# A decoder layer whose up projection uses pairs with seven products: another order of a pair's splits and products, and other distances between the additions and relus that close a column chunk

## The chip, the cores and the metric

The kernel runs on one core of one Trainium2 chip. The metric is the device time of the core in microseconds (us). Before the change it is 1089.05 us, the median of three runs (1088.41 to 1090.12).

## The reference, cut to what matters

One decoder layer on x of 256 tokens x 2048 channels, in float32:

```python
h = rmsnorm(x) * norm_attn_pre
p = h @ w_in                       # q, k, v of A; two latents and the shared key of B
A = dilated_window_attention(...)  # 8 heads of 128
B = causal_attention(...)          # 8 heads, from the latents by w_uq and w_ukv
x = x + rmsnorm(concat(A, B) @ w_out) * norm_attn_post
h = rmsnorm(x) * norm_mlp_pre
u = square(relu(h @ w_up))         # 2048 -> 8192
x = x + rmsnorm(u @ w_down) * norm_mlp_post   # 8192 -> 2048
```

The change lies in the line with w_up.

## The kernel before, in words

**Exact products from parts.** Every float32 operand is split into two parts of TensorE's format, `hi` (rounded by ScalarE, L268, or L272 where a gain is multiplied in) and `lo` (the rest, subtracted by VectorE, L269 or L273). A product of two operands is three matmuls into one PSUM bank: hi by hi, hi by lo, lo by hi (`three`). Both token blocks have 128 tokens. A matmul holds 128x128 of the tokens' side still and streams 512 weight columns.

**The weight stream.** All weights of the program lie in one list of tiles, 128 rows x 1024 columns (512 KB) at most. `Weights.get` keeps the splits six tiles ahead of the tile that TensorE is at. Loads go out on SyncE's queue into five buffers named `raw` (also `raw_w`), the split tiles into eight buffers `hi` and eight `lo`. A `raw` buffer is free again when the last `lo` that reads it is through VectorE, and the next load in the program's order takes the buffer that came free first; a `hi` buffer is free when TensorE's last matmul on it is done.

**The up projection.** It goes by eight chunks j of 1024 columns. A chunk has four accumulators, `acc_u` with index (b, n): token block b by column half n. Chunk 0 has 16 plain steps: one tile, twelve matmuls. Each later chunk has ten plain steps (k = 6 to 15) and three pairs ("w" in `UP_STEPS`), each over two of the k blocks 0 to 5. The steps stand as k6 to k10, pair 0, k11, k12, pair 1, k13, pair 2, k14, k15. A pair is a 2x2 by 2x2 block product done with seven products in place of eight. Its weights come as two raw tiles, a and b (`raw_w`), from which VectorE forms two tiles of sums, u and t (L314 to L317, `sums()`, tag `T` with two buffers). Four tiles of parts are made of them: `b11` (half of a), u, t and b. The seven products are 21 matmuls: four go to banks of their own (`m1`, `m6`, `m7`, `m5`, the banks of the chunk before), three right into `acc_u`.

**The end of a chunk.** After the last pair, `close` copies m1 (ScalarE, L871) and makes four corrections `c` of the m banks (four additions on VectorE, L874); this frees the banks, which the next chunk's accumulators take. Then `up_evac` runs for each of the four accumulators, beside the next chunk's first steps: an addition of c into `acc_u` (VectorE, L810), the relu into a tile `r` (ScalarE, L813), four transposes into `rt` (TensorE, L262), the square into `uT` (ScalarE, L821).

**What sets the order.** All engines run their instructions in the order in which the program is written, and it is written by a generator: `flow.pump()` stands after each product, and an evacuation goes on when the planned time that it last yielded has passed. `UP_STEP` is the planned distance between the four evacuations, the number after the addition that from addition to relu, `D_UP` that from relu to transposes. So these three numbers are no waits on the chip: they set between which instructions of ScalarE, VectorE and TensorE the addition, relu, transposes and square stand. The splits take their places by the weight stream's rule: a tile is split when TensorE's program gets to the tile six before it.

After the up projection comes the down projection (`y`), 1536 matmuls of the same kind.

Of the kernel before, what the change touches and what calls it, by code (L numbers as in the profile page):

```python
# [90 lines left out]
D_X0, D_X, D_SS, D_TAB = 6.0, 1.0, 3.0, (16.0, 20.0)  # L91
D_NORM, D_HT, D_SECOND = 4.5, 1.5, 4.0

D_UP, UP_STEP = 1.6, 2.1


N_SEVEN, SUMS_AHEAD = 3, 2
# [128 lines left out]
def layer(nc, tc, io):  # L226
    flow = Flow()

    def pool(name, side, **kw):
        return tc.alloc_tile_pool(name=name, bufs=1, side=side, **kw)  # L230
# [9 lines left out]
    def bank(i, name):  # L240
        return ps.tile([P, 512], F32, tag=f"bank{i}", bufs=1, name=name)
# [5 lines left out]
    def acc_bank(name):  # L247
        return next_bank(0, 4, name)
# [12 lines left out]
    def transpose(out, a):  # L261
        nc.tensor.transpose(out, a, ident)  # L262
        flow.spend(TR)

    def split(hi, lo, src, g=None):
        if g is not None:
            return split_gain(hi, lo, src, g)
        nc.scalar.activation(hi, src, AF.Copy)  # L268
        nc.vector.tensor_tensor(out=lo, in0=src, in1=hi.bitcast(F32), op=OP.subtract)  # L269

    def split_gain(hi, lo, src, g):
        nc.scalar.activation(hi, src, AF.Copy, scale=g)  # L272
        nc.vector.scalar_tensor_tensor(  # L273
            out=lo, in0=src, scalar=g, in1=hi.bitcast(F32), op0=OP.mult, op1=OP.subtract)

    def tok(t, k, b):
        return t[:, k, b * P:(b + 1) * P]

    weights = Weights(nc, wp, split, W_BUFS, W_AHEAD)
# [21 lines left out]
    def up_weight(j, k):  # L301
        return io["w_up"][k * P:(k + 1) * P, j * CW:(j + 1) * CW]
# [3 lines left out]
    def seven(j, kp):  # L306


        st, tt, H = {}, nc.vector.tensor_tensor, 512

        def sums():
            a, b = st["a"], st["b"] = [weights.load(up_weight(j, 2 * kp + i), CW, f"raw_w{j}_{kp}{i}") for i in range(2)]
            t, u = st["t"], st["u"] = [late["up"].tile([P, CW], F32, tag="T", bufs=2, name=f"{n}{j}_{kp}") for n in "tu"]
            tt(out=t[:, H:], in0=b[:, H:], in1=a[:, H:], op=OP.subtract)  # L314
            tt(out=u[:, :H], in0=t[:, H:], in1=a[:, :H], op=OP.add)
            tt(out=u[:, H:], in0=b[:, :H], in1=u[:, :H], op=OP.subtract)
            tt(out=t[:, :H], in0=a[:, H:], in1=a[:, :H], op=OP.subtract)  # L317

        def b11(hi, lo):
            split(hi[:, :H], lo[:, :H], st["a"][:, :H])  # L320

        return sums, [b11] + [lambda hi, lo, n=n: split(hi, lo, st[n]) for n in "utb"]

    wide_u = []
    for j in range(FF // CW):
        wide_u.append([])
        for what, k in [("k", k) for k in range(KD)] if j == 0 else UP_STEPS:
            if what == "k":  # L330
                ts = [weights.plan(up_weight(j, k), 1, CW, gcol[:, 8 + k:9 + k])]
            else:
                sums, fs = seven(j, k)
                weights.first[len(weights.specs) - SUMS_AHEAD] = sums
                ts = [weights.plan(f) for f in fs]
            wide_u[j].append((what, k, ts))
    down = []
    for g in range(FF // 512):
# [3 lines left out]
    def in_order(n, apart=(0, 0)):  # L342

        f, l = apart[0], n - apart[1]
        return ([(t, b) for b in range(NB) for t in range(f)] + [(t, b) for t in range(f, l) for b in range(NB)]
                + [(t, b) for b in range(NB) for t in range(l, n)])
# [327 lines left out]
    for what, ch in ch_b:  # L674
# [8 lines left out]
        else:  # L683
# [4 lines left out]
            after = [kr_chain, k_chain[pr]] + ([pair_chain[pr - 1]] if pr else [])  # L688
# [83 lines left out]
    def h_done(k, b):  # L772
        flow.until(lambda: 4 * parts[b] > k)

    res = [None] * NB
    for ns in ((0, 1), (2,), (3,)):
# [4 lines left out]
        for c, b, acc in proj(mixT, [ch_o[n] for n in ns], f"o{ns[0]}", order, heads_done):  # L781
            n = ns[c]
# [23 lines left out]
    def up_evac(j, b, i, acc, order, more=None):  # L806

        yield UP_STEP * order
        if more is not None:
            nc.vector.tensor_tensor(out=acc, in0=acc, in1=more, op=OP.add)  # L810
            yield 0.8
        r = late["up"].tile([P, 512], F32, tag="r", bufs=2, name=f"r{j}_{b}")
        nc.scalar.activation(r, acc, AF.Relu, scale=rstd2[b])  # L813
        yield D_UP
        t = bank(i, f"rt{j}_{b}")
        for k in range(4):
            transpose(t[:, k * P:(k + 1) * P], r[:, k * P:(k + 1) * P])
        if j not in uT:
            tag = {"tag": "T", "bufs": 2} if j >= 14 else {}
            uT[j] = late["up"].tile([P, CW], F32, name=f"uT{j}", **tag).rearrange("p (k s) -> p k s", k=4)  # L820
        nc.scalar.activation(uT[j][:, :, b * P:(b + 1) * P], t.rearrange("p (k s) -> p k s", k=4), AF.Square)  # L821
# [10 lines left out]
    sums = []  # L832
# [23 lines left out]
    def all_sums():  # L856
        for kp in range(N_SEVEN):
            yield from left_sums(kp)

    def three(out, a, w, first, last):  # L860

        for i, (x, y) in enumerate(((0, 0), (0, 1), (1, 0))):
            mm(out, a[x], w[y], first and i == 0, last and i == 2)
# [16 lines left out]
    for j in range(FF // CW):  # L880
        at = {bn: 4 * (j % 2) + i for i, bn in enumerate(PARTS)}
        if j == 0:
            accs = {bn: acc_bank(f"acc_u0_{bn[0]}{bn[1]}") for bn in at}
            at = {bn: (turn[0] - 3 + i) % 4 for i, bn in enumerate(at)}
        else:
            accs = {bn: bank(i, f"acc_u{j}_{bn[0]}{bn[1]}") for bn, i in at.items()}
        steps = wide_u[j]
        order = in_order(len(steps), (APART[1], 0)) if j == 0 else [(t, b) for t, (w, _, _) in enumerate(steps)
                                                                    for b in range(NB if w == "k" else 1)]
        for t, b in order:  # L890
            what, k, tiles = steps[t]
            if (j, t, b) == (0, 8, 0):
                flow.finish(*res)
                late["po"].release()
                mix.release()
                late["up"] = pool("up", "right")
                s_chain = flow.start(all_sums())
            if (j, t, b) == (FF // CW - 1, 4, 0):
                weights.limit -= 1
                u_next = split_u(0)  # L900
            if j == 1 and what == "w":
                flow.until(lambda: len(sums) > k)
            if what == "k":
                w = weights.get(tiles[0])
                h_done(k, b)
                for n in range(2):
                    c = slice(n * 512, (n + 1) * 512)
                    three(accs[b, n], [tok(hT[x], k, b) for x in range(2)], [w[x][:, 0, c] for x in range(2)], t == 0, t == len(steps) - 1)
                    if j == 0 and t == len(steps) - 1:
                        evac.append(flow.start(up_evac(n, b, at[b, n], accs[b, n], 2 * b + n - 0.25 * (2 * b + n))))  # L910
                    flow.pump()
                if b == NB - 1:
                    weights.free(tiles[0])
                continue

            first, last = k == 0, k == N_SEVEN - 1
            if first:
                m = {n: bank(i, f"m{n}_{j}") for n, i in zip((1, 6, 7, 5), free)}
            s1, s2, s3, s4 = sums[k]
            a11, a12, a22 = [[tok(hT[x], 2 * k + kk, bb) for x in range(2)] for kk, bb in ((0, 0), (1, 0), (1, 1))]  # L920
            prods = ((a11, 0, 0, 1), (s2, 1, 0, 6), (a22, 1, 1, (1, 0)), (s3, 2, 1, 7), (s1, 2, 0, 5),
                     (a12, 3, 0, (0, 0)), (s4, 3, 1, (0, 1)))
            for p, (a, i, half, to) in enumerate(prods):
                w = weights.get(tiles[i])
                out = m[to] if isinstance(to, int) else accs[to]
                three(out, a, [w[x][:, half * 512:half * 512 + 512] for x in range(2)],
                      isinstance(to, int) and first, isinstance(to, int) and last)
                if p == 6 or prods[p + 1][1] != i:
                    weights.free(tiles[i])
                flow.pump()  # L930
            if last:
                more = {}
                c_chain = flow.start(close(j, m, more))
        free = [at[bn] for bn in PARTS]
        if j:
            flow.finish(c_chain)
            for o, (b, n) in enumerate(PARTS):
                evac.append(flow.start(up_evac(2 * j + n, b, at[b, n], accs[b, n], o + 0.1, more[b, n])))
# [143 lines left out]
```

## Time and profile before

| what | value |
|---|---|
| median of three runs | 1089.05 us |
| the profiled execution's own time | 1087.93 us |
| its span, first to last instruction | 1086.1 us |
| around the span | 1.83 us |
| granted TensorE clock, mean | 0.996 |
| VectorE busy | 703.8 us, 65% of the span |
| ScalarE busy | 571.7 us, 53% of the span |
| up projection, about | 355 to 726 us of the span |
| down projection, about | 726 to 1074 us of the span |

The profile is of one execution. A view by lines gives groups of instructions, with busy time, the mean of one, and the idle time of the engine ahead of them with what ended it. A view of waits gives, for an engine, who was waited for, the sum in us, the number of times and the longest. A timeline gives for each instruction its start and its duration in us; a bracket behind it holds the engine's idle time ahead of it and what ended that. TensorE's instructions overlap, so the distance between starts, not the duration, is what one costs.

### The profile page before, as it was taken

The page shows a single profiled execution, that of the slowest core. Times are in us where ns is not written, and L with a number is a line of the kernel's source. Part 1 is how long each engine was busy: PE and PEld are TensorE (multiplying, and loading weights), DVE is VectorE, ACT ScalarE, POOL GpSimd, SP SyncE. Part 2 cuts the span into 40 slices and gives each one's busy share as a digit, 9 for nine tenths or more (in the row PEclk, how much of TensorE's full clock was granted, in tenths as well). Part 3 has the DMA queues.
Part 4 walks back from the last instruction along what each step waited for, and adds up shares of the span by engine and source line. Part 5 has one row for each costly group of instructions (what it writes and reads, how often), then busy time and mean ns, then how long its engine had stood idle before and what let it go on. Part 6 is the DMA issues. An engine that isn't in the chain of part 4 may idle for free.

```text
span 1086.1 us, 13207 instructions
## 1 busy us (share of the span) xinstructions
PE 1061.0 (98%) x4915; PEld 875.9 (81%) x4915; DVE 703.8 (65%) x927; ACT 571.7 (53%) x763; POOL 8.6 (1%) x18
## 2 busy tenths in 40 slices
PE   9999999999999989999999999999999999999997
PEld 6888899888888778787877878777888888888885
DVE  6586447477565796787887888875544454446444
ACT  6665446556463746565655656555444444444442
POOL 0000000000000000000000000000000000000000
PEclk9999999999999999999999999999999999999999
DMA  9885446454275564554646557375655655585532
GB/s 310 297 275 143 151 135 211 147 169 158 95 263 163 196 213 143 204 190 160 230 129 222 171 164 233 130 257 181 199 195 194 194 193 194 193 310 194 192 122 77
DMA packets 74303, 206.23 MB, mean 190 GB/s; under 512 B 6912, under 2 KB 11520, under 8 KB 73856
## 3 DMA queue, kind: packets, MB, share of 16 engines
q1 hardware_dynamic: 73520, 202.93, 57.1%
q10 hardware_dynamic: 720, 2.47, 0.7%
q8 instruction: 38, 0.62, 0.3%
q14 instruction: 25, 0.20, 0.1%
HBM read 201.18 MB, written 4.19 MB: 189 GB/s over the span
## 4 chain that ended last, share of the span: by engine, by line
PE 79%; DVE 10%; DMA 4%; ACT 4%; issue 3%; POOL 0%; DVEq 0%; POOLq 0%; ACTq 0%
PE y L258 31%; PE acc_u L258 12%; PE acc_o L258 8%; PE acc_k L258 4%; PE acc_v L258 4%; PE acc_q L258 4%; DVE lo L273 3%; PE m L258 3%; DVE lo L269 2%; PE acc_ckv L258 2%; DMA raw<-in_w_up 2%; PE acc_ukv L258 2%; PE acc_cq L258 2%; DVE c L874 2%; PE acc_uq L258 2%
## 5 line engine op out<-in xcount | busy, mean ns | idle before, releaser
L269 DVE TENSOR_TENSOR lo<-raw,hi 128x1024 fp32r<-128x1024 f32 (+3 forms) x253 | 293.0, 1165 | 245.9 <-ACT hi L268 243.8
L268 ACT ACTIVATE hi<-raw 128x1024 fp32r<-128x1024 f32 (+3 forms) x253 | 253.0, 1010 | 234.8 <-PE y L258 178.7
L258 PE MATMUL y<-hi,uhi 128*128 128x512 f32 x512 | 199.5, 390 | 0.4 <-DVE c L874 0.4
L258 PE MATMUL y<-lo,uhi 128*128 128x512 f32 x512 | 199.2, 389 | 0.0
L258 PE MATMUL y<-hi,ulo 128*128 128x512 f32 x512 | 160.3, 389 | 0.0
L258 PE MATMUL acc_u<-hi,hT_hi 128*128 128x512 f32 x386 | 155.2, 402 | 4.2 <-DVE c L874 4.1
L258 PE MATMUL acc_u<-hi,hT_lo 128*128 128x512 f32 x386 | 151.1, 391 | 0.4 <-DVE hT_lo L269 0.4
L258 PE MATMUL acc_u<-lo,hT_hi 128*128 128x512 f32 x386 | 151.0, 391 | 0.0
L272 ACT ACTIVATE hi<-raw,gcol 128x1024 fp32r<-128x1024 f32 x86 | 97.9, 1150 | 45.8 <-DMA raw<-in_w_up 29.3
L273 DVE SCALAR_TENSOR_TENSOR lo<-raw,gcol,hi 128x1024 fp32r<-128x1024 f32 x86 | 108.8, 1281 | 18.7 <-ACT hi L272 18.1
L258 PEld LDWEIGHTS y<-hi,uhi 128*128 128x128 f32 x512 | 96.1, 188 | 20.9 <-DVE c L874 1.1
L258 PEld LDWEIGHTS y<-hi,ulo 128*128 128x128 f32 x512 | 96.1, 188 | 20.1
L258 PEld LDWEIGHTS y<-lo,uhi 128*128 128x128 f32 x512 | 96.1, 188 | 19.9
L258 PEld LDWEIGHTS acc_u<-hi,hT_hi 128*128 128x128 f32 x386 | 72.8, 189 | 23.4 <-DVE c L874 7.8
L258 PEld LDWEIGHTS acc_u<-hi,hT_lo 128*128 128x128 f32 x386 | 72.7, 188 | 16.3 <-DVE hT_lo L269 0.9
L258 PEld LDWEIGHTS acc_u<-lo,hT_hi 128*128 128x128 f32 x386 | 72.9, 189 | 13.6
L258 PE MATMUL acc_o<-hi,mixT_hi 128*128 128x512 f32 x128 | 51.8, 405 | 0.0
L258 PE MATMUL acc_o<-hi,mixT_lo 128*128 128x512 f32 x128 | 50.2, 392 | 0.0
L258 PE MATMUL acc_o<-lo,mixT_hi 128*128 128x512 f32 x128 | 50.0, 390 | 0.0
L269 DVE TENSOR_TENSOR lo<-raw_w,hi 128x512 fp32r<-128x512 f32 (+1 forms) x42 | 40.0, 952 | 11.2 <-ACT hi L268 11.2
L813 ACT ACTIVATE r<-acc_u,rstd_pre 128x512 f32<-128x512 f32 x32 | 21.9, 689 | 45.3 <-DVE acc_u L810 43.2
L269 DVE TENSOR_TENSOR lo<-t,hi 128x1024 fp32r<-128x1024 f32 x21 | 25.7, 1223 | 19.6 <-ACT hi L268 19.5
(246 smaller groups left out, 1503.5 us busy)
## 6 DMA issues: line engine op xcount, KB each, us to landing
raw<-in_w_down SPq DMA_DIRECT2D x128, 512.0 KB, 4.6
raw<-in_w_up SPq DMA_DIRECT2D x86, 512.0 KB, 4.6
raw<-in_w_in SPq DMA_DIRECT2D x55, 512.0 KB, 5.0
raw_w<-in_w_up SPq DMA_DIRECT2D x42, 512.0 KB, 3.7
raw<-in_w_out SPq DMA_DIRECT2D x32, 512.0 KB, 4.3
raw<-in_w_in SPq DMA_DIRECT2D x16, 288.0 KB, 2.8
raw<-in_w_ukv SPq DMA_DIRECT2D x8, 512.0 KB, 4.9
raw<-in_w_uq SPq DMA_DIRECT2D x8, 384.0 KB, 3.3
```

The source lines that it names most:

```text
L258: nc.tensor.matmul(out, a, b, start=start, stop=stop)
L268: nc.scalar.activation(hi, src, AF.Copy)
L269: nc.vector.tensor_tensor(out=lo, in0=src, in1=hi.bitcast(F32), op=OP.subtract)
L272: nc.scalar.activation(hi, src, AF.Copy, scale=g)
L273: nc.vector.scalar_tensor_tensor(out=lo, in0=src, scalar=g, in1=hi.bitcast(F32), op0=OP.mult, op1=OP.subtract)
L813: nc.scalar.activation(r, acc, AF.Relu, scale=rstd2[b])
L874: tt(out=c[out], in0=m[x], in1=c[y], op=OP.add)
```

## The change

Three things differ.

1. The four tiles of a pair are split in the order a's half, b, u, t, where it was a's half, u, t, b.
2. The seven products follow: m1 (a's half), then the two products on b that go into `acc_u` (0,0) and (0,1), then the two on u, then the two on t. To keep the list consistent, a pair's `sums()` now come no earlier than behind the last split of the pair before.
3. The planned distances of the evacuations grow: addition to relu from 0.8 to 1.6, relu to transposes (`D_UP`) from 1.6 to 1.8, one evacuation to the next (`UP_STEP`) from 2.1 to 2.2.

```diff
-D_UP, UP_STEP = 1.6, 2.1
+D_UP, UP_STEP = 1.8, 2.2
...
-        return sums, [b11] + [lambda hi, lo, n=n: split(hi, lo, st[n]) for n in "utb"]
+        return sums, [b11] + [lambda hi, lo, n=n: split(hi, lo, st[n]) for n in "but"]
...
-    wide_u = []
+    wide_u, after = [], 0
...
                 sums, fs = seven(j, k)
-                weights.first[len(weights.specs) - SUMS_AHEAD] = sums
+                weights.first[max(len(weights.specs) - SUMS_AHEAD, after)] = sums
                 ts = [weights.plan(f) for f in fs]
+                after = len(weights.specs)
...
             nc.vector.tensor_tensor(out=acc, in0=acc, in1=more, op=OP.add)
-            yield 0.8
+            yield 1.6
...
-            prods = ((a11, 0, 0, 1), (s2, 1, 0, 6), (a22, 1, 1, (1, 0)), (s3, 2, 1, 7), (s1, 2, 0, 5),
-                     (a12, 3, 0, (0, 0)), (s4, 3, 1, (0, 1)))
+            prods = ((a11, 0, 0, 1), (a12, 1, 0, (0, 0)), (s4, 1, 1, (0, 1)), (s2, 2, 0, 6), (a22, 2, 1, (1, 0)),
+                     (s3, 3, 1, 7), (s1, 3, 0, 5))
```

What this moves is shown at the seam between chunk 3 and chunk 4; the seams behind chunks 1 to 6 all read alike. In the names, `r6_0` and `rt6_0` are the relu and the transposes of the accumulator (0,0) of chunk 3, `r7_0` of (0,1), `r6_1` of (1,0), `r7_1` of (1,1); `hi209` and so on are split tiles, numbered along the weight stream; `raw_w4_00` and `raw_w4_01` are a and b of chunk 4's pair 0, `u4_0` and `t4_0` its sums.

TensorE before, from the first to the second group of transposes at this seam:

```order
L262 MATMUL rt6_0_4861<-ident_84,r6_0_4843 128x128 x4
L258 MATMUL acc_u4_11_4825<-hi204_4735,hT_hi_2855 128x512
L258 MATMUL acc_u4_11_4825<-lo204_4736,hT_hi_2855 128x512
L258 MATMUL acc_u4_11_4825<-hi204_4735,hT_lo_2856 128x512
L258 MATMUL acc_u4_00_4822<-hi205_4747,hT_hi_2855 128x512
L258 MATMUL acc_u4_00_4822<-lo205_4748,hT_hi_2855 128x512
L258 MATMUL acc_u4_00_4822<-hi205_4747,hT_lo_2856 128x512
L262 MATMUL rt7_0_4879<-ident_84,r7_0_4859 128x128 x4
```

And TensorE in the changed kernel, at the same place:

```order
L262 MATMUL rt6_0_4864<-ident_84,r6_0_4850 128x128 x4
L258 MATMUL acc_u4_00_4822<-hi205_4747,hT_hi_2855 128x512
L258 MATMUL acc_u4_00_4822<-lo205_4748,hT_hi_2855 128x512
L258 MATMUL acc_u4_00_4822<-hi205_4747,hT_lo_2856 128x512
L258 MATMUL acc_u4_01_4823<-hi205_4747,hT_hi_2855 128x512
L258 MATMUL acc_u4_01_4823<-lo205_4748,hT_hi_2855 128x512
L258 MATMUL acc_u4_01_4823<-hi205_4747,hT_lo_2856 128x512
L258 MATMUL acc_u4_10_4824<-hi205_4747,hT_hi_2855 128x512
L258 MATMUL acc_u4_10_4824<-lo205_4748,hT_hi_2855 128x512
L258 MATMUL acc_u4_10_4824<-hi205_4747,hT_lo_2856 128x512
L262 MATMUL rt7_0_4885<-ident_84,r7_0_4862 128x128 x4
```

The first transposes stand three matmuls later (behind `acc_u4_11` of that step), and between the first and the second group stand nine matmuls instead of six, so the second group stands six matmuls later in all. Between the third and the fourth group, too, there are nine instead of six; between the second and the third nine, as before.

ScalarE before, at the same seam, from the split of pair 0's second tile on (`uT` are the squares):

```order
L268 ACTIVATE hi209_4826<-u4_0_4762 128x1024
L813 ACTIVATE r6_0_4843<-acc_u3_00_4446,rstd_pre20_3344 128x512
L268 ACTIVATE hi210_4845<-t4_0_4761 128x1024
L813 ACTIVATE r7_0_4859<-acc_u3_01_4447,rstd_pre20_3344 128x512
L821 ACTIVATE uT6_4866<-rt6_0_4861 128x4x128
L268 ACTIVATE hi211_4872<-raw_w4_01_4759 128x1024
L821 ACTIVATE uT7_4884<-rt7_0_4879 128x4x128
L813 ACTIVATE r6_1_4886<-acc_u3_10_4448,rstd_pre21_3439 128x512
L813 ACTIVATE r7_1_4898<-acc_u3_11_4449,rstd_pre21_3439 128x512
```

And ScalarE in the changed kernel:

```order
L268 ACTIVATE hi209_4826<-raw_w4_01_4759 128x1024
L268 ACTIVATE hi210_4843<-u4_0_4762 128x1024
L814 ACTIVATE r6_0_4850<-acc_u3_00_4446,rstd_pre20_3344 128x512
L814 ACTIVATE r7_0_4862<-acc_u3_01_4447,rstd_pre20_3344 128x512
L822 ACTIVATE uT6_4869<-rt6_0_4864 128x4x128
L268 ACTIVATE hi211_4872<-t4_0_4761 128x1024
L822 ACTIVATE uT7_4890<-rt7_0_4885 128x4x128
L814 ACTIVATE r6_1_4892<-acc_u3_10_4448,rstd_pre21_3439 128x512
L272 ACTIVATE hi212_4910<-raw212_4908,gcol_69 128x1024
L814 ACTIVATE r7_1_4920<-acc_u3_11_4449,rstd_pre21_3439 128x512
```

The split `hi210` moved ahead of the relu `r6_0`, and `hi212` ahead of `r7_1`. VectorE's instructions keep their places at this seam: `lo208`, four corrections, `lo209`, addition (0,0), `lo210`, additions (0,1) and (1,0), `lo211`, addition (1,1); only what `lo209` to `lo211` read is other, as on ScalarE.

VectorE before, at chunk 3's pair 2, between the two plain steps around it:

```order
L273 SCALAR_TENSOR_TENSOR lo196_4636<-raw196_4633,gcol_69,hi196_4635 128x1024
L269 TENSOR_TENSOR lo197_4652<-raw_w3_20_4613,hi197_4651 128x512
L269 TENSOR_TENSOR lo198_4668<-u3_2_4618,hi198_4667 128x1024
L269 TENSOR_TENSOR lo199_4675<-t3_2_4617,hi199_4674 128x1024
L269 TENSOR_TENSOR lo200_4685<-raw_w3_21_4615,hi200_4684 128x1024
L273 SCALAR_TENSOR_TENSOR lo201_4697<-raw201_4694,gcol_69,hi201_4696 128x1024
```

And VectorE in the changed kernel:

```order
L273 SCALAR_TENSOR_TENSOR lo196_4636<-raw196_4633,gcol_69,hi196_4635 128x1024
L269 TENSOR_TENSOR lo197_4652<-raw_w3_20_4623,hi197_4651 128x512
L269 TENSOR_TENSOR lo198_4668<-raw_w3_21_4625,hi198_4667 128x1024
L269 TENSOR_TENSOR lo199_4675<-u3_2_4628,hi199_4674 128x1024
L269 TENSOR_TENSOR lo200_4685<-t3_2_4627,hi200_4684 128x1024
L273 SCALAR_TENSOR_TENSOR lo201_4697<-raw201_4694,gcol_69,hi201_4696 128x1024
```

The raw tile b (`raw_w3_21`) is read by its last `lo` two splits earlier. The order of the loads on SyncE's queue is the same in both kernels, the count of instructions on every engine too, and from the end of chunk 7 on ScalarE, VectorE and TensorE have the same order in both.

## The prediction

> **What bounds the kernel now.** I read the page first, then TensorE's waits, then the timelines of one seam between two chunks. The page's head, its line of TensorE, and the granted clock in 40 slices of the span:
>
> ```profile
> span 1086.1 us, 13207 instructions
> PE 1061.0 (98%) x4915; PEld 875.9 (81%) x4915; DVE 703.8 (65%) x927; ACT 571.7 (53%) x763; POOL 8.6 (1%) x18
> PEclk9999999999999999999999999999999999999999
> ```
>
> TensorE is the bound: busy 98%, its clock granted at nine tenths or more in every slice. The change has the same matmuls as before, so only what TensorE waits can move. In the chain that ended last, one stretch of the down projection shows what a matmul costs without any wait:
>
> ```profile
> 740.75 331.90 PE y L258 x1464
> ```
>
> 331.90 / 1464 = 0.2267 us from start to start. TensorE's waits over the whole span (us in total, times, longest):
>
> ```profile
> PE rt L262 <- ACT r L813: 10.1, 8, 3.1
> PE acc_u L258 <- DVE c L874: 4.1, 8, 1.7
> ```
>
> The same view for 500 to 700 us, which holds the seams behind chunks 2 to 6:
>
> ```profile
> PE rt L262 <- ACT r L813: 5.7, 5, 1.2
> ```
>
> So transposes wait for a relu once at each of these five seams, 5.7 / 5 = 1.14 us. The first and the last of the five in TensorE's timeline:
>
> ```profile
> 505.68 0.66 PE L262 MATMUL rt<-ident,r 128*128 128x128 f32 x4 [1.14 <-ACT r L813]
> 688.55 0.66 PE L262 MATMUL rt<-ident,r 128*128 128x128 f32 x4 [1.15 <-ACT r L813]
> ```
>
> They are alike to 0.01 us: a wait made by the order, not by chance. TensorE at the seam between chunks 3 and 4 (start, duration):
>
> ```profile
> 543.00 0.39 PE L258 MATMUL acc_u<-hi,hT_lo 128*128 128x512 f32 x1
> 543.51 0.50 PE L258 MATMUL acc_u<-hi,hT_hi 128*128 128x512 f32 x1
> ...
> 545.56 0.50 PE L258 MATMUL acc_u<-hi,hT_hi 128*128 128x512 f32 x1 [0.35 <-DVE c L874]
> ...
> 548.41 0.60 PE L262 MATMUL rt<-ident,r 128*128 128x128 f32 x4
> ...
> 550.00 0.40 PE L258 MATMUL acc_u<-hi,hT_lo 128*128 128x512 f32 x1
> 551.55 0.66 PE L262 MATMUL rt<-ident,r 128*128 128x128 f32 x4 [1.15 <-ACT r L813]
> ...
> 554.10 0.60 PE L262 MATMUL rt<-ident,r 128*128 128x128 f32 x4
> ```
>
> The second transposes, rt7_0, were due 0.23 behind the start at 550.00, at 550.23, and began at 551.55: the wait costs 1.32 us with the refilling of the pipeline. ScalarE there:
>
> ```profile
> 541.83 1.05 ACT L268 ACTIVATE hi<-u 128x1024 fp32r<-128x1024 f32 x1
> 547.27 0.69 ACT L813 ACTIVATE r<-acc_u,rstd_pre 128x512 f32<-128x512 f32 x1 [4.39 <-DVE acc_u L810]
> 547.86 1.05 ACT L268 ACTIVATE hi<-t 128x1024 fp32r<-128x1024 f32 x1
> 550.81 0.69 ACT L813 ACTIVATE r<-acc_u,rstd_pre 128x512 f32<-128x512 f32 x1 [1.90 <-DVE acc_u L810]
> ```
>
> And VectorE there:
>
> ```profile
> 540.97 1.28 DVE L273 SCALAR_TENSOR_TENSOR lo<-raw,gcol,hi 128x1024 fp32r<-128x1024 f32 x1 [0.61 <-ACT hi L272]
> 542.77 2.73 DVE L874 TENSOR_TENSOR c<-m,c 128x512 f32<-128x512 f32 x4
> 545.42 1.22 DVE L269 TENSOR_TENSOR lo<-u,hi 128x1024 fp32r<-128x1024 f32 x1
> 546.55 0.69 DVE L810 TENSOR_TENSOR acc_u<-acc_u,c 128x512 f32<-128x512 f32 x1
> 548.94 1.22 DVE L269 TENSOR_TENSOR lo<-t,hi 128x1024 fp32r<-128x1024 f32 x1 [1.70 <-ACT hi L268]
> 550.09 1.29 DVE L810 TENSOR_TENSOR acc_u<-acc_u,c 128x512 f32<-128x512 f32 x2
> ```
>
> Read the two together: it is a loop. The relu r6_0 (547.27) waits for addition (0,0); the split hi210 stands behind it (547.86 to 548.91); lo210 waits for hi210 (548.94); addition (0,1) stands behind lo210 (550.09); r7_0 waits for that addition (550.81 to 551.50); rt7_0 starts at 551.55. ScalarE lost 4.39 us ahead of r6_0, in which hi210 could have run.
>
> **Part 3 of the change, the distances: this carries the forecast.** In the changed order hi210 stands ahead of r6_0. It can follow hi209 (541.83 + 1.05 = 542.88); its output buffer is that of chunk 3's last tile, whose last matmul is the one at 543.00 at the latest (end 543.39). So it ends by 543.4 + 1.05 = 544.5, long before r6_0 can start at 547.27: no delay there. VectorE then goes through: addition (0,0) ends at 547.24, lo210 takes 1.22 to 548.46, addition (0,1) 0.69 to 549.15, r7_0 0.69 to about 549.9.
>
> When is it needed? rt6_0 stands three matmuls later: 548.41 + 0.68 = 549.09 (r6_0 ends at 547.96). From one group of transposes over nine matmuls to the next takes what 551.55 to 554.10 shows, 2.55. So rt7_0 is due at 549.09 + 2.55 = 551.64, and r7_0 is done at 549.9: 1.7 us to spare. Either move alone would do: at the old place the due time is 550.23, still behind 549.9. The wait goes at five seams: 5 x 1.32 = 6.6 us. Behind chunk 0 the 3.1 us are for the first relu, whose place does not change, and behind chunk 7 the order stays as it was: 0 at both. Behind chunk 1 the second transposes did not wait (no bracket), so 0 there too:
>
> ```profile
> 459.98 0.62 PE L262 MATMUL rt<-ident,r 128*128 128x128 f32 x4
> ```
>
> What is late next? r6_1 stands behind the square uT7, which waits for rt7_0. What this round trip takes is seen behind chunk 0, where ScalarE waited in the same order, TensorE's row first, then ScalarE's:
>
> ```profile
> 409.95 0.60 PE L262 MATMUL rt<-ident,r 128*128 128x128 f32 x4
> ```
>
> ```profile
> 410.59 0.60 ACT L821 ACTIVATE uT<-rt 128x512 f32<-128x512 f32 x1 [1.37 <-PE rt L262]
> 411.08 0.68 ACT L813 ACTIVATE r<-acc_u,rstd_pre 128x512 f32<-128x512 f32 x1
> ```
>
> Transposes to square 0.64, square to relu 0.49, relu to the transposes that wait for it 551.55 - 550.81 = 0.74: 1.87 in all, of the 2.55 to rt6_1. So rt6_1 (due 554.19) has 0.68 to spare. Then r7_1: r6_1 starts at 551.64 + 1.13 = 552.77, hi212 behind it about 0.6 later for 1.15 (as a gain split takes about what the 1.05 row takes), r7_1 to about 555.3; rt7_1 is due at 554.19 + 2.55 = 556.74: 1.4 to spare. Cost of both: 0, and what they could cost is the second rival.
>
> **Parts 1 and 2, splits and products.** A product on u takes as long as one on b, and tiles are used up in the same rhythm (one product, then two, two, two), so TensorE's sum is 0. The sums u and t are needed two products later than before, b earlier; b needs no more than its load, which the sums that stood first needed too: 0. `sums()` of pair 2 move behind one more split on VectorE; no wait is added, since VectorE does the same work before the plain tile behind it: 0.
>
> What they do change is when loads leave. b's buffer comes free earlier, and it goes to a later load. SyncE's issues ahead of the seam:
>
> ```profile
> 528.60 0.33 SPq L169 DMA_DIRECT2D raw<-in_w_up  x1
> ...
> 532.33 0.33 SPq L169 DMA_DIRECT2D raw<-in_w_up  x1
> 535.05 0.33 SPq L169 DMA_DIRECT2D raw<-in_w_up  x1
> ```
>
> And ScalarE's two splits that waited for the last two of these:
>
> ```profile
> 537.67 1.15 ACT L272 ACTIVATE hi<-raw,gcol 128x1024 fp32r<-128x1024 f32 x1 [2.93 <-DMA raw<-in_w_up]
> 539.78 1.15 ACT L272 ACTIVATE hi<-raw,gcol 128x1024 fp32r<-128x1024 f32 x1 [0.95 <-DMA raw<-in_w_up]
> ```
>
> The load at 528.60 takes the buffer of pair 2's b (its issue follows that lo, by the order in which buffers come free) and would leave two splits earlier, about 2 x 1.22 = 2.4 us. The two behind it landed after 537.67 - 532.33 = 5.34 and 539.78 - 535.05 = 4.73 us; with less ahead of them they may land sooner. The second one sets VectorE's row at 540.97 (0.61 idle), that the corrections at 542.77 to 545.50, and these TensorE's delays at 543.51 (543.51 - 543.00 - 0.23 = 0.28) and 545.56 (0.35). But the buffer of that load is not b's, so it leaves when it did. Bounds: 0, since its issue does not move, to 0.61 at each of the six seams behind chunks 1 to 6, 3.7 in all; not below 0, since no load leaves later. I take 0.1 a seam, near the low end, because the load that decides took only 4.73 already and left 2.7 us behind the one before: 0.5 us.
>
> A DMA has by the Trainium skill ("DMA: Bandwidth & Descriptors", Anatomy of one DMA) a fixed 2.0 us and then 436 GB/s, an estimate of 3.2 us for 512 KB alone. By that page the load with 4.73 us still stood in a queue and would gain all of the bound; the sum would be 6.6 + 3.7 = 10.3. The trace has no such load alone at that place, so this is a rival, with a small chance.
>
> **The sum.** 6.6 + 0.5 = 7.1 us. Against the profiled execution: 1087.93 - 7.1 = 1080.8 us. The median of the runs is 1089.05, 1.12 longer than that execution, for all of the program alike: 1089.05 - 7.1 = 1082.0 us.
>
> One thing stays as it is and can differ from run to run. Behind chunk 0 TensorE waits 3.12 us, and then its matmuls start 0.43 apart for a while:
>
> ```profile
> 405.95 1.12 PE L262 MATMUL rt<-ident,r 128*128 128x128 f32 x4 [3.12 <-ACT r L813]
> ...
> 407.71 0.63 PE L258 MATMUL acc_u<-hi,hT_lo 128*128 128x512 f32 x1
> 408.14 0.63 PE L258 MATMUL acc_u<-hi,hT_hi 128*128 128x512 f32 x1
> ```
>
> Behind the waits of 1.15 us there is no such stretch. The Trainium skill ("TensorE: Matmul & The Clock Gate", What's actually happening) says that the clock halves after an idle window of about 3.4 us, and that the window runs freely, so that a wait near that length may or may not trip it. The trace agrees in kind: 0.43 is about twice 0.2267. Some six matmuls x 0.2 = 1.2 us can thus be absent in another run; this widens the low end of the range, no more.
>
> **The rivals.**
>
> *More is gained (chance 0.10).* The closing chain moves up as well, by most of its 0.61 us a seam. For: four loads in 3.7 us crowd the queue. Against: the deciding load does not move. Time: 1089.05 - 6.6 - 3.7 = 1078.8.
>
> *A new wait takes a part (0.13).* rt6_1 comes to wait for r6_1 behind uT7, because hi211 on ScalarE gets in between. If it starts late and holds uT7 up by its own 1.05, 1.05 - 0.68 = 0.37 a seam over six seams, 2.2 us: 1082.0 + 2.2 = 1084.2. Against: hi211 starts behind uT6 near 550.4 and ends a microsecond before rt7_0's results.
>
> *The wait only moves (0.08).* If the weight stream, and not the relu, sets the pace, TensorE gets ahead by 1.3 us and loses it at the corrections c: 1089 us, no change. For: ScalarE does wait for loads. Against: the loads wait for buffers, which TensorE's progress frees, so they move with it.
>
> *Slower (0.04).* The sums of pair 2, now behind all four splits of pair 1, wait for their load, VectorE holds the splits behind them, and TensorE waits for the lo of k13 once a chunk. What lead that lo has in chunk 3 is in VectorE's timeline and in the chain that ended last, whose 18 matmuls are the last six of pair 1 and the twelve of k13:
>
> ```profile
> 522.03 1.28 DVE L273 SCALAR_TENSOR_TENSOR lo<-raw,gcol,hi 128x1024 fp32r<-128x1024 f32 x1
> ```
>
> ```profile
> 528.43 4.09 PE acc_u L258 x18
> ```
>
> k13 starts at 528.43 + 6 x 0.2267 = 529.79, and its lo is done at 523.31: 6.5 us of lead. With the sums 8.0 us late, seven chunks lose 1.5 us each: 1082.0 + 10.5 = 1092.5. It decides from 7.1 / 7 = 1.0 us a chunk, 7.5 us late, on. Nothing in SyncE's queue moves later, so I give it little.
>
> **How the numbers follow.** Forecast 0.65, the rest as above. What a measurement here can tell from no change is about 0.2%, 2.2 us: below 1086.9 is faster. Faster: 0.65 + 0.10 + 0.13 = 0.88; same 0.08; slower 0.04. The range goes from 1079.0 (most of the first rival, or the forecast without the slow stretch and with some of the closing chain) to 1086.0 (the second rival with 1.8 us for the spread of the runs); it leaves out the last two rivals and a little of the first.
>
> **What would show it.** Right: in 500 to 700 us TensorE's wait of transposes for relus gone, the addition (0,1) right behind lo210 without VectorE idling ahead of that split, waits on c within 0.2 us of before at each seam, the 3.12 us behind chunk 0 still there. Wrong: the 5.7 us reappear at rt6_1 or rt7_1, or under acc_u waiting for c; or a lo of a pair becomes what a matmul waits for.

## The result, and the profile after

The changed kernel takes 1079.95 us (median of 4 runs, 1078.4 to 1081.71), against 1089.59 for the kernel before beside it (4 runs). The ratio is 0.9912, 95% interval 0.989 to 0.9934. The forecast was 1082.0, a gain of 7.1 us; the gain against the kernel before beside it is 9.6. The profiled execution of the changed kernel took 1081.16 us. Its page, the head, TensorE's line and the granted clock:

```profile
span 1079.4 us, 13208 instructions
PE 1059.7 (98%) x4915; PEld 876.8 (81%) x4915; DVE 703.0 (65%) x927; ACT 573.5 (53%) x763; POOL 7.7 (1%) x18
PEclk9999999999999999999999999999999999999998
```

The same 4915 matmuls, the same clock: what went is waiting. TensorE's waits over the whole span (us in total, times, longest):

```profile
PE rt L262 <- ACT r L814: 4.6, 3, 3.3
PE acc_u L258 <- DVE c L875: 2.0, 5, 0.4
...
PE acc_u L258 <- ACT hi L268: 1.2, 1, 1.2
```

The 1.2 us put down to a split `hi` are one wait at the head of chunk 2, at a place where the kernel before waited 1.74 us for c. And from 500 to 700 us, the seams behind chunks 2 to 6, where the wait for a relu stood at 5.7, this is all that is left:

```profile
PE acc_u L258 <- DVE c L875: 1.7, 4, 0.4
```

The seam between chunks 3 and 4 can be held against the forecast step by step. TensorE's timeline (start, duration), the four groups of transposes:

```profile
544.43 0.50 PE L258 MATMUL acc_u<-hi,hT_hi 128*128 128x512 f32 x1 [0.42 <-DVE c L875]
...
547.99 0.60 PE L262 MATMUL rt<-ident,r 128*128 128x128 f32 x4
...
550.52 0.60 PE L262 MATMUL rt<-ident,r 128*128 128x128 f32 x4
...
553.03 0.60 PE L262 MATMUL rt<-ident,r 128*128 128x128 f32 x4
...
555.56 0.60 PE L262 MATMUL rt<-ident,r 128*128 128x128 f32 x4
```

No bracket on any of the four. ScalarE there:

```profile
542.02 1.06 ACT L268 ACTIVATE hi<-u 128x1024 fp32r<-128x1024 f32 x1 [0.33 <-ACT hi L268]
546.16 0.69 ACT L814 ACTIVATE r<-acc_u,rstd_pre 128x512 f32<-128x512 f32 x1 [3.08 <-DVE acc_u L811]
547.89 0.69 ACT L814 ACTIVATE r<-acc_u,rstd_pre 128x512 f32<-128x512 f32 x1 [1.05 <-DVE acc_u L811]
...
551.65 0.68 ACT L814 ACTIVATE r<-acc_u,rstd_pre 128x512 f32<-128x512 f32 x1
...
553.26 0.69 ACT L814 ACTIVATE r<-acc_u,rstd_pre 128x512 f32<-128x512 f32 x1
```

And VectorE:

```profile
545.43 0.69 DVE L811 TENSOR_TENSOR acc_u<-acc_u,c 128x512 f32<-128x512 f32 x1
546.03 1.22 DVE L269 TENSOR_TENSOR lo<-u,hi 128x1024 fp32r<-128x1024 f32 x1
547.16 1.29 DVE L811 TENSOR_TENSOR acc_u<-acc_u,c 128x512 f32<-128x512 f32 x2
```

The loop is open. The split hi210 (542.02) stands in ScalarE's idle time ahead of the first relu, VectorE goes from the first addition through lo210 to the second without a bracket, and r7_0 is done at 547.89 + 0.69 = 548.58 for transposes at 550.52. The down projection then begins 6.7 us sooner and is as long as before:

```profile
734.04 331.92 PE y L258 x1464
```

### The profile page after: what moved, and what is told of

Its sections match the earlier page's. It is cut to its first block, busy times and chain, and to the rows that moved or that the text cites. A ratio compares the mean times of both kernels' runs of the same rounds, so it can differ in the third digit from the quotient of the medians.

```text
span 1079.4 us, 13208 instructions
## 1 busy us (share of the span) xinstructions
PE 1059.7 (98%) x4915; PEld 876.8 (81%) x4915; DVE 703.0 (65%) x927; ACT 573.5 (53%) x763; POOL 7.7 (1%) x18
## 4 chain that ended last, share of the span: by engine, by line
PE 85%; DVE 6%; DMA 4%; ACT 2%; issue 2%; POOL 0%; DVEq 0%; POOLq 0%; SPq 0%; ACTq 0%
PE y L258 32%; PE acc_u L258 17%; PE acc_o L258 8%; PE acc_k L258 4%; PE acc_v L258 4%; PE m L258 4%; PE acc_q L258 4%; DMA raw<-in_w_up 3%; PE acc_ckv L258 2%; DVE lo L273 2%; PE acc_ukv L258 2%; PE acc_cq L258 2%; PE acc_uq L258 2%; ACT hi L272 1%; DVE c L875 1%
## 5 line engine op out<-in xcount | busy, mean ns | idle before, releaser
L268 ACT ACTIVATE hi<-raw_w 128x512 fp32r<-128x512 f32 (+1 forms) x42 | 34.7, 840 | 24.2 <-PE acc_u L258 21.9
```

## The experiments

Eleven runs, nine of them timed beside the kernel before; two repeats without such timing follow further down. The first four of the table stood against that kernel at 1089.88 us (14 runs), the next four at 1089.13 (12 runs), apart_early at 1088.82 (7 runs).

| kernel | what differs | us (runs) | ratio to before, interval |
|---|---|---|---|
| after_again | the change | 1079.92 (5) | 0.9904 (0.9887 to 0.9921) |
| apart_only | distances alone | 1083.25 (6) | 0.994 (0.9927 to 0.9954) |
| order_only | splits and products alone | 1086.28 (8) | 0.9962 (0.9948 to 0.9975) |
| relu_late | relus later, transposes in place (behind chunk 0, which has no addition, transposes earlier) | 1086.57 (7) | 0.9974 (0.9962 to 0.9985) |
| trans_late | transposes later, relus in place | 1080.93 (5) | 0.9926 (0.9912 to 0.994) |
| splits_only | splits alone | 1085.58 (7) | 0.9967 (0.9955 to 0.9979) |
| early_close | the change, closing at once | 1074.03 (4) | 0.9855 (0.984 to 0.987) |
| early_close_j0 | that, chunk 0's end later | 1068.26 (4) | 0.9806 (0.9792 to 0.982) |
| apart_early | distances, closing at once | 1073.52 (4) | 0.9853 (0.9833 to 0.9873) |

**The two halves of the change.** The changed kernel again, its distances alone, and its order alone:

> The changed kernel once more, to size what is to be explained. Two theories on its gain of 9.6 us at the median (7.1 forecast). Theory A (two terms): the five waits of transposes for a relu, 6.6 us, and the corrections c coming earlier at the seams, about 1.3 us, make 7.9; the rest of the 9.6 is scatter of single runs ahead of the up projection. Then the median lies at 0.9918 to 0.9935 of the kernel before. Theory B: there is a third term of some 2 us that one trace does not show. Then it comes again at 0.9905 to 0.9915.

> Only part 3, the distances; splits and products in the old order. Theory A: the loop of addition, relu, split is broken by the distances alone: 6.6 us faster, about 0.994; between 500 and 700 us no wait of transposes for a relu, and the waits on c as before (2.0 us there). Rival C: the order of splits and products is needed for it: then less than half of that.

> Only parts 1 and 2, the order of splits and products; the old distances. Theory A: the five waits of 1.15 us stay, and the corrections c come 0.2 us earlier at each seam: 1.3 us faster, about 0.9988. The forecast had 0.5 us (0.9995). Rival C: the order breaks the loop by itself: 3 us or more faster, with the waits for relus smaller than 5.7 us between 500 and 700 us.

```diff
apart_only, against before:
-D_UP, UP_STEP = 1.6, 2.1
+D_UP, UP_STEP = 1.8, 2.2
...
-            yield 0.8
+            yield 1.6
order_only: the other lines of the change
```

The distances alone gain 1089.88 - 1083.25 = 6.6 us, the order alone 3.6, both 9.96: within the intervals they add up. In the stretch 500 to 700 us, apart_only shows

```profile
PE acc_u L258 <- DVE c L874: 3.3, 7, 0.7
```

and no wait for a relu; order_only shows the other half:

```profile
PE rt L262 <- ACT r L814: 5.6, 5, 1.2
PE acc_u L258 <- DVE c L875: 1.3, 3, 0.4
```

So the distances remove the five waits and the order leaves them. The waits for c do the opposite: 2.0 before, 3.3 with the distances alone (2.0 was expected), 1.3 with the order alone. After_again's ratio of 0.9904 lies just below both ranges that were expected of it, and order_only gains more than twice the 1.3 us of its first theory: what that theory lacks lies in the term of the order.

**Would either move alone do?** The forecast said so. Two kernels make one move each.

> The kernel before, with the distance from addition to relu 1.6 and that from relu to transposes 0.8 (their sum as it was) and the old distance between evacuations: the relu moves behind the split, the transposes stay where they were on TensorE. Theory A (the loop is broken by the relu's place, and the later transposes are spare): r7_0 is done at about 549.9 on the old clock of the seam, due at 550.23: no wait, 6.6 us faster, about 0.994. Rival D: the later transposes are needed, since the real lead is shorter than the 0.3 us worked out: a wait of some tenths remains at each seam, or more at the later groups, and the gain is below 5 us.

> Before with D_UP 2.95 in place of 1.6 and nothing else: the transposes of an evacuation stand two groups of three matmuls later, the relus stay where they were on ScalarE (r6_0, hi210, r7_0). The prediction said that either move alone would take the five waits away. Theory A: r7_0 is ready at about the same time as before and due 1.36 us later, so the five waits are gone (at most 0.3 us of them left in the stretch 500 to 700), and the time falls by 6.6 to 1083.3 (1082 to 1084.5), unless the end of chunk 7 takes part of it back as in relu_late. Rival E (the later transposes push the squares and with them the relus of the next bank later by as much): waits of the transposes for relu of 3 us or more stay in that stretch, 1087 to 1090.

```diff
relu_late:
-D_UP, UP_STEP = 1.6, 2.1
+D_UP, UP_STEP = 0.8, 2.1
...
-            yield 0.8
+            yield 1.6
trans_late:
-D_UP, UP_STEP = 1.6, 2.1
+D_UP, UP_STEP = 2.95, 2.1
```

In both, the waits for relus between 500 and 700 us are gone, so either move alone does it. But neither gains just the 6.6 us. Relu_late gains 3.3. Most of what it lacks lies behind chunk 7, where its last two relus each stand behind a square. TensorE there in the kernel before (transposes, then the down projection):

```profile
738.54 0.66 PE L262 MATMUL rt<-ident,r 128*128 128x128 f32 x4 [0.39 <-ACT r L813]
740.09 0.66 PE L262 MATMUL rt<-ident,r 128*128 128x128 f32 x4 [0.90 <-ACT r L813]
740.50 0.48 PE L258 MATMUL y<-hi,uhi 128*128 128x512 f32 x1
```

And in relu_late:

```profile
735.61 0.66 PE L262 MATMUL rt<-ident,r 128*128 128x128 f32 x4 [1.31 <-ACT r L813]
737.53 1.11 PE L262 MATMUL rt<-ident,r 128*128 128x128 f32 x4 [1.26 <-ACT r L813]
738.30 0.78 PE L258 MATMUL y<-hi,uhi 128*128 128x512 f32 x1
738.87 0.63 PE L258 MATMUL y<-lo,uhi 128*128 128x512 f32 x1
739.30 0.63 PE L258 MATMUL y<-hi,uhi 128*128 128x512 f32 x1
```

The waits grow by 2.57 - 1.29 = 1.3 us, and a stretch of slow matmuls follows (starts 0.43 apart) that the kernel before has not, some 1.3 us. Besides, its first wait behind chunk 0 is 3.58 us where it was 3.12, and the waits for c between 500 and 700 us are 2.7 where they were 2.0. Trans_late gains 8.2 us, more than expected, at the other end: behind chunk 0 its transposes stand later as well, so the first wait is shorter and no slow stretch follows (next start 0.41 behind the four transposes, as after any of them):

```profile
406.77 0.66 PE L262 MATMUL rt<-ident,r 128*128 128x128 f32 x4 [2.13 <-ACT r L813]
407.18 0.48 PE L258 MATMUL acc_u<-hi,hT_hi 128*128 128x512 f32 x1
```

That is 3.12 - 2.13 = 1.0 us and about 1.4 us of slow matmuls. Against this its waits for c between 500 and 700 us grew from 2.0 to 3.7 us: 6.6 + 2.4 - 1.7 = 7.3 of the 8.2.

**What the order gains by.** Splits_only has the queues of SyncE, ScalarE and VectorE of order_only, and TensorE's old order of products.

> Before with the splits in the order a, b, u, t (as in the changed kernel) but the seven products in the old order (those of b last), old distances. The queues of SP, ACT and DVE stand as in order_only; only TensorE's own order differs from it. Theory A (order_only's gain of 3.6 us comes from b's raw buffer coming free two splits earlier, so that loads land and corrections run earlier): the time of order_only, 1086.3 (1085 to 1087), and in the stretch 500 to 700 us the waits for c fall from 2.0 to about 1.3 us while the waits of the transposes for relu stay at about 5.6. Rival P (the gain comes from the order of the products, which asks for u's and t's tiles later): 1089.9 (1088.5 to 1091), waits for c about 2.0. Rival H (b's finished tile, now held to the pair's end, keeps later splits back): slower than before by 1 us or more, with waits of acc_u for hi.

> splits_only, unchanged, for a second profile: its profiled execution was the slowest of its 7 runs (1088.72 against a median of 1085.58) and showed a stretch of slow matmuls of about 2.6 us behind the first transposes of chunk 0. An execution near the median should show that stretch at about 1.3 us or less, and waits for c of no more than 1.8 us in the stretch 500 to 700.

```diff
splits_only, against order_only:
-            prods = ((a11, 0, 0, 1), (a12, 1, 0, (0, 0)), (s4, 1, 1, (0, 1)), (s2, 2, 0, 6), (a22, 2, 1, (1, 0)),
-                     (s3, 3, 1, 7), (s1, 3, 0, 5))
+            prods = ((a11, 0, 0, 1), (s2, 2, 0, 6), (a22, 2, 1, (1, 0)), (s3, 3, 1, 7), (s1, 3, 0, 5),
+                     (a12, 1, 0, (0, 0)), (s4, 1, 1, (0, 1)))
```

1085.58 us, a gain of 3.55, as much as order_only's 3.6: by the times, the order of the splits carries it, and that of the products little. Its first profile (of its slowest run, 1088.72 us) shows 1.8 us of waits for c in 500 to 700 us, where 1.3 was expected; the second (one run, 1087.37 us) shows 1.4. The relu waits are 5.7 in both:

```profile
PE acc_u L258 <- DVE c L875: 1.4, 5, 0.4
```

The second profile's slow stretch behind chunk 0 was 1.6 us and not the 1.3 expected.

Whether corrections really come earlier is read from ScalarE. In each seam one split waits for TensorE, and the closing's copy of m1 stands four instructions behind it. The pair in the seam between chunks 3 and 4, in the kernel before:

```profile
532.55 2.19 ACT L272 ACTIVATE hi<-raw,gcol 128x1024 fp32r<-128x1024 f32 x2 [1.56 <-PE acc_u L258]
...
540.84 0.58 ACT L871 ACTIVATE c<-m 128x512 f32<-128x512 f32 x1
```

And in the changed kernel:

```profile
531.77 2.20 ACT L272 ACTIVATE hi<-raw,gcol 128x1024 fp32r<-128x1024 f32 x2 [1.52 <-PE acc_u L258]
...
539.64 0.58 ACT L872 ACTIVATE c<-m 128x512 f32<-128x512 f32 x1
```

8.29 us before, 7.87 after. The mean over the six seams behind chunks 1 to 6 is 8.20 and 8.15 in the two profiles of the kernel before, 8.39 in apart_only, 8.05 and 7.90 in the two of splits_only, 7.68 in order_only, 7.85 in the changed kernel and 7.83 in after_again. So the new order brings the copy, and the corrections behind it, 0.3 to 0.55 us forward at each seam, 1.8 to 3.3 us over six.

What moved it is one load. In the kernel before, SyncE issued the load that takes b's buffer at 528.60 (the prediction shows the row), 3.95 us ahead of that split. In the changed kernel it goes out 7.48 us ahead of it:

```profile
524.29 0.33 SPq L169 DMA_DIRECT2D raw<-in_w_up  x1
```

It is so at all six seams, 3.95 us before and 7.47 or 7.48 after, and the loads behind it go out at the same distance from the split as before, to 0.05 us. They only land sooner: on average over the six, the split that stands last before the copy starts 6.80 us behind the marked one, where it was 7.14.

**Is that all the order does?** If so, it is worth nothing once the corrections are out of the way. Early_close moves them there: copy and corrections go out at once, ahead of the next splits, so that they no longer stand behind a split that waits for its load. Apart_early does that with the old order.

> The changed kernel with the closing of a chunk's products issued at once: the copy c0 and the four corrections stand ahead of the next splits on ScalarE and VectorE instead of between them. Theory A (what is left at the seams are the first matmuls' waits for a correction that stands behind a split which waits for its load): the waits for c are gone, 4 to 5 us less than the changed kernel, 1075.5 (1074.5 to 1077). Rival F (the splits behind them come late instead: five operations of VectorE, 2.8 us by the four additions in the row, now stand ahead of lo207): waits of acc_u for hi or lo take their place, 1079 to 1082.

> The kernel before with the new distances (as apart_only) and with the closing issued at once (as early_close); the order of the splits and of the products is the old one. Only parts 1 and 2 of the change stand between this kernel and early_close. Theory A (all that the new order gains runs through the corrections' lateness at the seams): with the corrections out of the way the order is worth nothing, so this is as fast as early_close, 1074.0 (1073 to 1075), with no waits for c or hi in the stretch 500 to 700. Rival O (the order gains by another way as well, up to the 3.3 us that lie between apart_only and the changed kernel): 1076 to 1077.5, or waits of acc_u for hi or lo that early_close does not have.

```diff
-        yield 1.0
         nc.scalar.activation(c[0], m[1], AF.Copy)
-        yield 0.7
...
-            yield 0.7
+            yield 0.0
...
                 c_chain = flow.start(close(j, m, more))
+                flow.pump()
```

1074.03 (a little below its range) and 1073.52 us: with the new order and with the old one, the same within the spread of runs. In both, nothing is left for TensorE to wait for between 500 and 700 us; the only waits for relus left are behind chunks 0 and 7. Over the whole span early_close shows

```profile
PE rt L262 <- ACT r L814: 4.1, 3, 2.8
```

and apart_early

```profile
PE rt L262 <- ACT r L813: 4.7, 3, 3.4
```

So no gain of the order is left once the corrections come early. Where TensorE waits for nothing, none could show; but in apart_only, too, TensorE waits for nothing but c between 500 and 700 us, so there the order's gain can only come from these waits. The corrections' lateness cost 1083.25 - 1073.52 = 9.7 us in the old order (two sessions, whose kernels before differ by 1.06 us; by the ratios 9.5) and 1079.95 - 1074.03 = 5.9 in the new one (by the ratios 6.2): a difference of 3.3 to 3.8, about what order_only measured.

**The end of chunk 0, and a faster kernel.**

> early_close, and the evacuations of chunk 0 start 1.6 steps of the order (3.5 us) later, so that their transposes stand about fifteen matmuls further on. Theory A: the wait of the first transpose behind chunk 0 (3.1 to 3.3 us in the pages) goes, and with it the stretch of slow matmuls behind it (about 1.2 us): 4.5 us less than early_close, 1071 (1069.5 to 1073). Rival G (the wait is only handed on: the first matmuls that reuse these banks, or the products of chunk 1 that need the sums, wait as long): the time of early_close within 1 us.

```diff
-    ... up_evac(n, b, at[b, n], accs[b, n], 2 * b + n - 0.25 * (2 * b + n))))
+    ... up_evac(n, b, at[b, n], accs[b, n], 2 * b + n - 0.25 * (2 * b + n) + 1.6)))
```

1068.26 us, 11.7 less than the changed kernel and 20.9 less than the kernel before; that is 5.8 less than early_close, 1.3 more than expected. The wait behind chunk 0 is nearly gone, and the slow matmuls with it:

```profile
407.45 0.66 PE L262 MATMUL rt<-ident,r 128*128 128x128 f32 x4 [0.22 <-ACT r L814]
407.86 0.48 PE L258 MATMUL acc_u<-hi,hT_hi 128*128 128x512 f32 x1
```

Not handed on: over the whole span TensorE's waits for relus are 1.5 us, mostly at the end of chunk 7.

```profile
PE rt L262 <- ACT r L814: 1.5, 3, 0.9
```

**How much single profiles differ.**

> The kernel before, unchanged, for a second profile: its first profiled execution took 1087.93, 1.1 to 2 us less than the medians of its runs (1089.05 to 1089.88). If the waits for c differ from execution to execution, the slower execution shows more than the 2.0 us that the first showed in the stretch 500 to 700 (6 waits), at waits for relu that stay at 5.7. If they don't, the difference lies ahead of the up projection or in the stretch of slow matmuls behind the first transposes of chunk 0.

One run, 1088.95 us. From 500 to 700 us it agrees with the first profile to 0.1 us:

```profile
PE rt L262 <- ACT r L813: 5.7, 5, 1.1
PE acc_u L258 <- DVE c L874: 2.0, 6, 0.4
```

So these waits came alike in both executions. Of the 1.0 us between the two profiled executions, 0.7 lies ahead of the first transposes of chunk 0, which begin at 405.95 in the first and at 406.63 here.

The gain at the seams can be measured apart from such scatter: from the first matmul of chunk 1's pair 0 to that of chunk 7's pair 0 lie the six seams behind chunks 1 to 6. In before_again:

```profile
423.44 0.39 PE L258 MATMUL m<-hi,hT_hi 128*128 128x512 f32 x1
...
697.65 0.39 PE L258 MATMUL m<-hi,hT_hi 128*128 128x512 f32 x1
```

And in apart_only:

```profile
422.84 0.39 PE L258 MATMUL m<-hi,hT_hi 128*128 128x512 f32 x1
...
691.79 0.39 PE L258 MATMUL m<-hi,hT_hi 128*128 128x512 f32 x1
```

| kernel | six seams, us (each from one profile) |
|---|---|
| before, before_again | 274.56, 274.21 |
| apart_only | 268.95 |
| order_only | 272.26 |
| splits_only, splits_again | 273.64, 272.84 |
| changed kernel, after_again | 266.34, 266.29 |
| apart_early | 260.78 |
| early_close | 260.38 |

By this the distances are worth 5.3 to 5.6 us at the seams, the order alone 1.9 to 2.3 and on top of the distances 2.6, the whole change 7.9 to 8.3. The gains by the medians are 0.7 to 2 us larger; no profile shows where that lies.

## Why the prediction was right, and where it was not

**The five waits: right in kind, and in size for the waits themselves.** Forecast 5 x 1.32 = 6.6 us from the distances, and the five waits are gone. That apart_only gains just 6.6 by the times (5.0 to 8.0 by the interval) is in part luck: with the distances alone the waits for c grew by 3.3 - 2.0 = 1.3 us, and by its profile the five seams behind chunks 2 to 6 got shorter by 228.6 - 223.25 = 5.3 us, which is 6.6 less 1.3. The steps hold in the seam shown: nine matmuls between groups took 550.52 - 547.99 = 2.53 (forecast 2.55); r7_0 was done 550.52 - 548.58 = 1.9 us ahead of its transposes (1.7); r6_1, done at 552.33, 0.7 ahead of those at 553.03 (0.68); r7_1, done at 553.95, 1.6 ahead of those at 555.56 (1.4). No delay of the first relu came from hi210, which ended at 543.08 (forecast by 544.5), 3.1 us ahead of the relu.

**"Either move alone would do": right for these five seams, not for the time.** It left out that the same three numbers also place the ends of chunks 0 and 7, where they are worth about -3 us (relu_late: 2.6 behind chunk 7, 0.5 behind chunk 0) and about +2.4 us (trans_late). And in both the waits for c grew. In the change itself the two moves leave these ends as they were: 0.39 and 0.9 us behind chunk 7 in both, 3.12 and 3.35 behind chunk 0.

**The order of splits: the mechanism right, the size wrong.** This is the term that was mis-sized: bounds 0 to 0.61 a seam, "I take 0.1 a seam, near the low end", 0.5 us in all. It measured 3.6 us alone and 3.3 on top of the distances (1083.25 - 1079.92); the copy came 0.3 to 0.55 us sooner a seam, half of the bound or more. The premise held: the deciding load does not leave earlier (2.50 us behind the split that waits for TensorE, in both kernels). But it does not bear the low end, since the load ahead left 7.48 - 3.95 = 3.5 us sooner (forecast 2.4) and this one then took less time to land. Its issue and the split that waited for it, in the changed kernel:

```profile
534.27 0.33 SPq L169 DMA_DIRECT2D raw<-in_w_up  x1
```

```profile
538.59 1.15 ACT L272 ACTIVATE hi<-raw,gcol 128x1024 fp32r<-128x1024 f32 x1 [0.81 <-DMA raw<-in_w_up]
```

4.32 us, where it was 4.73. The Trainium skill ("DMA: Bandwidth & Descriptors", Anatomy of one DMA) gives 2.0 us and 436 GB/s for the gpsimd path, an estimate of 3.2 us for such a load alone; these loads go out on SyncE's queue, so the figure is for another path than theirs, and the trace's 4.32 us lie above it. In the prediction the sum by that page was 10.3 and the time 1078.8; the measured 1079.95 lies nearer to this rival than to the forecast.

**The rivals.** No new wait came at rt6_1, and nothing got slower. That the wait only moves to the corrections was true for a small part, the 1.3 us of the distances alone, and the order took that back: 1.7 us of waits for c are left in 500 to 700 us.

**What stays open.** The profiles place 7.9 to 8.3 us of the whole gain at the six seams, where the medians give 9.6 to 10.0; the rest no profile places, and single executions of one kernel differ by more. For the order alone the profiles place 1.9 to 2.3 of 3.6 us. Nor is it settled what the order of the products adds: nothing by splits_only's time, but by the profiles the six seams are 0.6 to 1.4 us shorter in order_only than in splits_only.

## What to carry to other kernels

Where the order of in-order engines is written by a generator, a wait that returns in each round to 0.01 us may well come from a place in the order and not from a lack of speed: draw the loop over the engines, and look which instruction could stand in idle time ahead of it. What closes a round and frees banks belongs ahead of work that may wait for a load: that alone was worth more here (5.9 to 9.7 us) than the order's 3.6. A load can land sooner without leaving sooner: look at what is ahead of it in the queue. And a number that sets distances acts at every seam, so cost it at the first and the last too.

## What the runs showed of the hardware

The prediction took the slow stretch behind chunk 0 for something that can be absent in another run. In all eleven profiles in which TensorE waited there 2.78 to 3.6 us it came: four to ten matmuls start 0.4 us or more apart, mostly 0.43. After 2.13 (trans_late) and 0.22 us (early_close_j0) none do. In the kernel before the granted clock is 0.50 from 406.7 to 409.0 us and 1.00 from 409.5 to 412. The shortest wait that such a stretch followed, in early_close:

```profile
407.02 0.98 PE L262 MATMUL rt<-ident,r 128*128 128x128 f32 x4 [2.78 <-ACT r L814]
...
408.65 0.63 PE L258 MATMUL acc_u<-hi,hT_lo 128*128 128x512 f32 x1
409.07 0.63 PE L258 MATMUL acc_u<-hi,hT_hi 128*128 128x512 f32 x1
```

In relu_late it also followed two waits of 1.31 and 1.26 us with eight small transposes directly ahead of them and four between; the granted clock is 0.52 from 737.5 to 740.5. The Trainium skill ("TensorE: Matmul & The Clock Gate", What's actually happening) puts the idle window after which the clock halves at about 3.4 us; here less than that was enough. And in apart_only the stretch begins only 1.4 us after the wait is over:

```profile
405.67 0.66 PE L262 MATMUL rt<-ident,r 128*128 128x128 f32 x4 [2.92 <-ACT r L813]
...
407.46 0.63 PE L258 MATMUL acc_u<-hi,hT_lo 128*128 128x512 f32 x1
407.89 0.63 PE L258 MATMUL acc_u<-hi,hT_hi 128*128 128x512 f32 x1
```

which would fit a window that runs freely, as that page has it. Measured from these transposes to the sixteenth matmul behind them (4.39 us in trans_late), the stretch cost 1.3 to 1.6 us beside the wait in ten of the eleven profiles, and 2.7 in the first of splits_only.
